# Building the gate table of a 128 x 128 expert grid: one-hot rows by Relu on ACT in place of compares on DVE

## The chip, the core and the metric

The kernel runs on one core of one Trainium2 chip. The metric is the device time in microseconds of one execution. TensorE appears in the profile as PE (matmuls) and PEld (weight loads), VectorE as DVE, ScalarE as ACT, GpSimd as POOL and SyncE, which only issues transfers, as SP.

## The reference, cut to what matters

One decoder layer is computed for 1024 prompt rows and 64 sample rows: norm, input projection, a recurrent branch and a windowed attention branch, a merge, an output projection, and then an expert layer with 8 heads that pick 16 experts each out of 128 x 128:

```python
s_top, i_top = lax.top_k(s, PEER_TOPK)                    # 16 of 128 keys on each of two axes
cand = s_top[:, :, 0, :, None] + s_top[:, :, 1, None, :]  # 16 x 16 sums
cand_idx = i_top[:, :, 0, :, None] * N_KEYS + i_top[:, :, 1, None, :]
best, pos = lax.top_k(cand, PEER_TOPK)
idx = jnp.take_along_axis(cand_idx, pos, axis=-1)         # expert numbers, 128 per token
g = jax.nn.softmax(best, axis=-1)                         # gates
act = jax.nn.gelu(jnp.einsum('cd,ced->ce', xc, expert_u[ic])) * gc
return jnp.einsum('ce,ced->cd', act, expert_v[ic])
```

For 704 of the 1088 tokens the kernel computes this layer densely, over all 16384 experts. For this it needs a gate table per token: a 128 x 128 array that holds the gate at row i, column j where expert 128 i + j was picked, and zero elsewhere.

## The kernel before

The rows are worked in three blocks: 320 rows (256 prompt and 64 sample rows), 384 and 384. A block goes through `trunk`: attention, gate and attention-branch projections (with `mg`), the recurrent part `lru`, its branch projection, the output projection `w_out`, the second norm (whose transposes on PE write the PSUM tile `tr`), and `retrieve`, which computes the key scores and the two top-16 lists. What a block's lists need after that is background work, done while the next block is in `trunk`: `choose` (top 16 of the candidate sums, expert numbers, softmax) and, for the first two blocks alone, `build_g`, which makes the gate tables. The 384 rows of the third block are gathered expert by expert during `dense`, the last and longest part (from 1912 us on), which reads the tables of the other 704 tokens.

The background work is a Python generator. `bg(k)` takes k steps of it at set places of `trunk` (`PG1` and `PG2` list how many), and so sets its place in the order of the program; a scheduler then orders each engine's queue. All tiles of one name share a ring of buffers that is given out in the order of the program. The PSUM tile `tr` has three buffers, used by the table products, by the key scores and by every transpose, those of the second norm too. A step of `build_g` makes the tables of four tokens, called a group here; 80 groups are built during the second block and 96 during the third.

A group before: DVE compares a row of the numbers 0 to 127 with the tokens' column numbers (line 889) and row numbers (line 890), giving one-hot rows for 4 tokens x 128 slots. The gate is held as a sum of three bf16 parts, so the row one-hots are multiplied by each part (line 891 on POOL, 892 and 893 on DVE). PE multiplies the one-hots, three 128 x 128 bf16 matmuls per token that add up in `tr` (lines 896 to 898), and ACT copies the result into `sg` (line 899). After eight groups (32 tokens) `sg` is stored to `g_d` with 2 MB (line 901). `sg` has one buffer.

In `choose`, line 786 compares 50 candidate places with the 16 picked places, POOL multiplies by the expert numbers (line 788), DVE adds up (line 789). In attention, line 443 scales the softmax on POOL. Weights come by SP (`wraw`), are split into a high part by ACT (`whi`, line 148) and a low part by POOL (`wlo`, line 149), and go to PE.

## Time and profile before

| what | value |
|---|---|
| median of 3 runs | 4001.42 us (3998.14 to 4010.92) |
| the profiled execution's own time | 3999.96 us |
| its span, from the first to the last instruction | 3998.0 us |
| PE busy | 3641.4 us, 91% of the span |
| DVE busy | 3151.0 us, 79% |
| POOL busy | 2407.2 us, 60% |
| ACT busy | 1290.8 us, 32% |

Busy time is summed over the whole span and so is a mean of stages with different limits. The first block lasts from 0 to 520 us, the second to 1232, the third to 1912, and `dense` to the end. The two middle stretches are 1392 us long, and the background work lies in them. A matmul's recorded duration includes the filling of the array, so several overlap; what one costs is read from one start to the next.

### The profile page before, as it was taken

Reading aid. Unit: us, or ns where it says so; the run is one execution under the profiler, and the core shown is the slowest. Engines: PE = TensorE matmul, PEld = TensorE weight load, DVE = VectorE, ACT = ScalarE, POOL = GpSimd, SP = SyncE. Lnnn points to the kernel's source line nnn. Section 1 sums busy time; section 2 is a strip of 40 time slices with the busy share of each in tenths; the row PEclk is TensorE's granted clock in tenths of the full one; section 3 lists DMA queues with packets and bytes.
Section 4 is the critical chain, followed back from the end, with each engine's and each line's share of the span. In section 5 each row is a group of like instructions: output and inputs, shape, how many; then the busy total and the mean of one; then the engine's idle time right before and its main releaser. Section 6 shows DMA issues by size and latency. Waiting matters only on the chain. (4 is left out here: it accounts for less than half of the span.)

```text
span 3998.0 us, 60600 instructions
## 1 busy us (share of the span) xinstructions
PE 3641.4 (91%) x22734; PEld 3477.6 (87%) x22734; DVE 3151.0 (79%) x6798; ACT 1290.8 (32%) x2346; POOL 2407.2 (60%) x1560
## 2 busy tenths in 40 slices
PE   7988998778897878998899999999999999999998
PEld 6778978668895777888799999999999999999998
DVE  6365787999899988998987777777777777777773
ACT  4454353443333435333222222222222222222221
POOL 3444546565554664764576677767766767676651
PEclk8989999889997988999899999999999999999999
DMA  5334523234441133444359898999989899899972
GB/s 148 100 111 149 154 72 90 79 101 145 171 139 56 58 94 108 138 173 162 125 204 308 292 318 303 321 323 316 322 295 311 306 319 316 309 317 310 319 259 80
DMA packets 505654, 821.75 MB, mean 206 GB/s; under 512 B 34220, under 2 KB 360812, under 8 KB 502000
## 3 DMA queue, kind: packets, MB, share of 16 engines
q1 hardware_dynamic: 394768, 415.18, 32.5%
q0 software_dynamic: 110592, 402.70, 28.2%
q8 instruction: 178, 2.92, 0.3%
q14 instruction: 116, 0.95, 0.1%
HBM read 753.25 MB, written 66.50 MB: 205 GB/s over the span
## 5 line engine op out<-in xcount | busy, mean ns | idle before, releaser
L149 POOL TENSOR_TENSOR wlo<-wraw,whi 128x1024 fp32r<-128x1024 f32 x252 | 639.3, 2544 | 513.7 <-ACT whi L148 476.0
L168 PE MATMUL ou<-ah,vh 128*128 128x352 f32 x2048 | 663.4, 327 | 40.6 <-ACT ah L148 23.3
L168 PE MATMUL sc<-dx,uh 128*128 128x352 f32 x2048 | 664.6, 325 | 16.2 <-ACT uh L148 9.0
L169 PE MATMUL ou<-al,vh 128*128 128x352 f32 x2048 | 660.1, 325 | 5.3 <-DVE al L149 5.0
L170 PE MATMUL sc<-dx,ul 128*128 128x352 f32 x2048 | 662.0, 323 | 1.0 <-POOL ul L149 1.0
L169 PE MATMUL sc<-dx,uh 128*128 128x352 f32 x2048 | 662.5, 324 | 0.0
L170 PE MATMUL ou<-ah,vl 128*128 128x352 f32 x2048 | 659.0, 324 | 0.0
L859 DVE SCALAR_TENSOR_TENSOR acc<-row,hv,acc 128x1024 f32<-128x1024 f32 x384 | 493.1, 1284 | 157.3 <-DMA row<-in_expert_v,iA 151.6
L847 DVE SCALAR_TENSOR_TENSOR row<-row,xt 128x1024 f32<-128x1024 f32 x384 | 465.5, 1217 | 174.3 <-DMA row<-in_expert_u,iA 165.0
L857 POOL DMA_INDIRECT row<-in_expert_v,iA x384 | 362.2, 943 | 267.8 <-DVE acc L859 192.6
L845 POOL DMA_INDIRECT row<-in_expert_u,iA x384 | 362.4, 944 | 264.4 <-DVE row L847 187.4
L168 PEld LDWEIGHTS ou<-ah,vh 128*128 128x128 f32 x2048 | 385.0, 189 | 55.7 <-ACT ah L148 29.7
L168 PEld LDWEIGHTS sc<-dx,uh 128*128 128x128 f32 x2048 | 386.9, 189 | 20.0 <-DVE al L149 9.8
L148 ACT CAST whi<-wraw 128x1024 fp32r<-128x1024 f32 x252 | 263.9, 1049 | 429.6 <-PE mm L169 167.6
L169 PEld LDWEIGHTS ou<-al,vh 128*128 128x128 f32 x2048 | 387.0, 189 | 7.8 <-DVE al L149 7.8
L170 PEld LDWEIGHTS sc<-dx,ul 128*128 128x128 f32 x2048 | 386.5, 189 | 1.4 <-POOL ul L149 1.4
L169 PEld LDWEIGHTS sc<-dx,uh 128*128 128x128 f32 x2048 | 387.2, 189 | 0.0
L170 PEld LDWEIGHTS ou<-ah,vl 128*128 128x128 f32 x2048 | 386.8, 189 | 0.0
L970 DVE TENSOR_TENSOR dac<-dac,ou 128x352 f32<-128x352 f32 x672 | 339.3, 514 | 59.9 <-PE ou L170 58.0
L149 POOL TENSOR_TENSOR vl<-vn,vh 128x1024 fp32r<-128x1024 f32 x128 | 309.0, 2422 | 65.6 <-ACT vh L148 38.5
L149 POOL TENSOR_TENSOR ul<-un,uh 128x1024 fp32r<-128x1024 f32 x128 | 310.7, 2427 | 45.7 <-ACT uh L148 43.6
L891 POOL TENSOR_TENSOR oij<-oij,s 128x512 bf16<-128x512 bf16 x176 | 225.1, 1290 | 176.9 <-DVE oij L890 132.7
(287 smaller groups left out, 8484.5 us busy)
## 6 DMA issues: line engine op xcount, KB each, us to landing
wraw<-in_w_in SPq DMA_DIRECT2D x132, 512.0 KB
un<-in_expert_uT SPq DMA_DIRECT2D x128, 512.0 KB
vn<-in_expert_v SPq DMA_DIRECT2D x128, 512.0 KB
g_d<-sg SPq DMA_DIRECT2D x22, 2048.0 KB
gt<-g_d SPq DMA_DIRECT2D x64, 704.0 KB
wraw<-in_peer_w_query SPq DMA_DIRECT2D x48, 512.0 KB
wraw<-in_w_branch_attn SPq DMA_DIRECT2D x24, 512.0 KB
wraw<-in_w_branch_lru SPq DMA_DIRECT2D x24, 512.0 KB
```

The lines of the kernel that those rows point to most:

```text
L148: nc.scalar.copy(hi, src)
L149: return (lo_eng or nc.vector).tensor_tensor(lo, src, f32(hi), op=ALU.subtract)
L168: nc.tensor.matmul(ps, lh, rh, start=first and j == 0, stop=False)
L169: nc.tensor.matmul(ps, lh, rl, start=False, stop=False)
L170: nc.tensor.matmul(ps, ll, rh, start=False, stop=last and j == n - 1)
L845: nc.gpsimd.indirect_dma_start(out=row, out_offset=None, in_=i["expert_u"], in_offset=bass.IndirectOffsetOnAxis(ap=ia[:, s:s + 1], axis=0))
L847: nc.vector.scalar_tensor_tensor(row, row, 1.0, xt, op0=ALU.mult, op1=ALU.mult, accum_out=hv[:, s:s + 1])
L857: nc.gpsimd.indirect_dma_start(out=row, out_offset=None, in_=i["expert_v"], in_offset=bass.IndirectOffsetOnAxis(ap=ia[:, s:s + 1], axis=0))
L859: nc.vector.scalar_tensor_tensor(acc, row, hv[:, s:s + 1], acc, op0=ALU.mult, op1=ALU.add)
L891: nc.gpsimd.tensor_tensor(wl, wh, col(4), op=ALU.mult)
L970: nc.vector.tensor_tensor(ac[k // 4][:, k % 4, a:b], ac[k // 4][:, k % 4, a:b], ps[:, 0:b - a], op=ALU.add)
```

## The change

The one-hot rows are no longer compared on DVE. For a slot with number s and a column c, the squared distance (s - c)^2 is written as a product of eight factors of s by eight factors of c, split so that each factor is exact in bf16. The slots' factors go to DRAM (`ft_d`), are read back eight tokens at a time with the eight factors on partitions (`fq`), and PE multiplies them by a constant 8 x 256 table (`fcmp`): 256 columns of distances per token, for the column and the row number. ACT then computes Relu(1 - d) for the column one-hots, and Relu(w - w d) for the row one-hots, with the gate w as a pointer operand for scale and for bias. One fp32 matmul per token multiplies both. The product of a group is issued after the distances of the next one. `choose` finds the expert number as the least of |32768 place + number - 32768 wanted|, with a subtract and a reduce on DVE and nothing on POOL. The softmax scaling in attention is four ACT instructions in place of one on POOL. Setup builds the constant table and takes it through DRAM.

```diff
+        row = self.sp.tile([1, NF, 2, P], BF16, tag="s4", name="row", bufs=N4)
...
+        nc.sync.dma_start(self.fc_d.rearrange("(o f) x c -> o f x c", o=1), row)
+        self.fcmp = c.tile([NF, 2 * P], BF16, name="fcmp")
+        nc.sync.dma_start(self.fcmp, self.fc_d.rearrange("f x c -> f (x c)"))
...
-            nc.gpsimd.tensor_tensor(sb[:, :, 0:S], sb[:, :, 0:S], z4.unsqueeze(2).to_broadcast([P, 4, S]), op=ALU.mult)
+            for g in range(4):
+                nc.scalar.activation(sb[:, g, 0:S], sb[:, g, 0:S], AF.Copy, scale=z4[:, g:g + 1])
...
+            nc.vector.tensor_tensor(ce[0:r], ce[0:r], self.iota[0:r].unsqueeze(1).to_broadcast([r, PH, NCAND]), op=ALU.add)
...
-                nc.vector.tensor_tensor(eq[0:r], self.iota[0:r].unsqueeze(1).to_broadcast([r, TOPK, NCAND]),
-                                        bf[0:r, h].unsqueeze(2).to_broadcast([r, TOPK, NCAND]), op=ALU.is_equal)
-                nc.gpsimd.tensor_tensor(eq[0:r], eq[0:r], ce[0:r, h].unsqueeze(1).to_broadcast([r, TOPK, NCAND]), op=ALU.mult)
-                nc.vector.tensor_reduce(ev[0:r, h], eq[0:r], axis=AX.X, op=ALU.add)
+                nc.vector.tensor_tensor(eq[0:r], ce[0:r, h].unsqueeze(1).to_broadcast([r, TOPK, NCAND]),
+                                        bf[0:r, h].unsqueeze(2).to_broadcast([r, TOPK, NCAND]), op=ALU.subtract)
+                nc.vector.tensor_reduce(ev[0:r, h], eq[0:r], axis=AX.X, op=ALU.min, apply_absolute_value=True)
...
+                nc.vector.tensor_scalar(x12[0:r, 0, 2], e32[0:r], 7, None, op0=ALU.arith_shift_right)
+                nc.vector.tensor_scalar(x12[0:r, 1, 2], e32[0:r], 127, None, op0=ALU.bitwise_and)
+                nc.vector.tensor_tensor(x12[0:r, :, 0], x12[0:r, :, 2], x12[0:r, :, 2], op=ALU.mult)
+                nc.vector.tensor_scalar(x12[0:r, :, 1], x12[0:r, :, 0], 127, None, op0=ALU.bitwise_and)
+                nc.vector.tensor_scalar(x12[0:r, :, 0], x12[0:r, :, 0], 7, None, op0=ALU.arith_shift_right)
+                nc.scalar.copy(fb[0:r, 0:6], x12[0:r].rearrange("p x f s -> p (x f) s"))
...
+                nc.sync.dma_start(self.ft_d[:, n0:n0 + r, :].rearrange("f n s -> n f s"), fb[0:r])
...
+        def product(ch, t4, sg, oij):
+            pt = self.tr()
+            for x in range(4):
+                nc.tensor.matmul(pt[:, x, :], oij[:, x, 1], oij[:, x, 0], start=True, stop=True)
+            nc.scalar.copy(sg[:, :, t4 * 4:t4 * 4 + 4], pt.rearrange("p x i -> p i x"))
+            if t4 == CH // 4 - 1:
+                nc.sync.dma_start(self.g_d[ch], sg)
...
-                nc.vector.tensor_tensor(oj, self.iota4, col(1), op=ALU.is_equal)
-                nc.vector.tensor_tensor(wh, self.iota4, col(0), op=ALU.is_equal)
-                nc.gpsimd.tensor_tensor(wl, wh, col(4), op=ALU.mult)
-                nc.vector.tensor_tensor(wm, wh, col(3), op=ALU.mult)
-                nc.vector.tensor_tensor(wh, wh, col(2), op=ALU.mult)
...
-                    nc.tensor.matmul(pt[:, x, :], oj[:, :, x], wh[:, :, x], start=True, stop=False)
-                    nc.tensor.matmul(pt[:, x, :], oj[:, :, x], wm[:, :, x], start=False, stop=False)
-                    nc.tensor.matmul(pt[:, x, :], oj[:, :, x], wl[:, :, x], start=False, stop=True)
...
+                    fq = sp.tile([NF, CF, NSLOT], BF16, tag="fq", name="fq", bufs=2)
+                    nc.sync.dma_start(fq, self.ft_d[:, n0:n0 + CF, :])
...
+                for x2 in range(2):
+                    ps = self.tr((P, 2, 2, P))
+                    for x in range(2):
+                        m = (t4 * 4) % CF + 2 * x2 + x
+                        nc.tensor.matmul(ps[:, x].rearrange("p a c -> p (a c)"), fq[:, m, :], self.fcmp, start=True, stop=True)
+                    nc.scalar.activation(oij[:, 2 * x2:2 * x2 + 2, 1, :], ps[:, :, 1, :], AF.Relu, scale=-1.0, bias=1.0)
+                    for x in range(2):
+                        m = t4 * 4 + 2 * x2 + x
+                        nc.scalar.activation(oij[:, 2 * x2 + x, 0, :], ps[:, x, 0, :], AF.Relu, scale=sw[:, 1, m:m + 1], bias=sw[:, 0, m:m + 1])
+                if late:
+                    product(*late.pop(0))
+                late.append((ch, t4, sg, oij))
                 yield
```

The order of the queues. First PE in the third block, where the last background groups meet the first transpose of the second norm (`xn`); `oij` are the one-hots, `tr` the shared PSUM tile. Before:

```order
L896 LDWEIGHTS oij_17693
L896 MATMUL tr_17699<-oij_17693 128x128
L897 LDWEIGHTS oij_17693
L897 MATMUL tr_17699<-oij_17693 128x128
L898 LDWEIGHTS oij_17693
L898 MATMUL tr_17699<-oij_17693 128x128
L239 MATMUL tr_17741<-ident_60,xn_17722 128x128 [waits DVE_49,Activation_49]
L239 MATMUL tr_17741<-ident_60,xn_17722 128x128 x3
```

Now, at the same place:

```order
L936 LDWEIGHTS fq_17566 [waits PE_49]
L936 MATMUL tr_17684<-fcmp_226,fq_17566 128x256 [waits Activation_49]
L936 LDWEIGHTS fq_17566
L936 MATMUL tr_17684<-fcmp_226,fq_17566 128x256
L912 MATMUL tr_17690<-oij_17568 128x128 [waits Activation_49]
L912 MATMUL tr_17690<-oij_17568 128x128 x3
L263 MATMUL tr_17724<-ident_60,xn_17705 128x128 [waits DVE_49,PE_49,Activation_49]
L263 MATMUL tr_17724<-ident_60,xn_17705 128x128 x3
```

Each pair of distance matmuls and each product now takes a buffer of `tr` and waits for ACT. Of the third block's 96 groups, 66 stood ahead of the first `w_out` matmul before and 30 between it and the retrieval; now 41 and 55, of which 43 stand back to back with no projection between. Of the second block's 80 groups, 30, 28 and 22 stood in the recurrent branch's projection, in `w_out` up to the retrieval, and in the retrieval; now 2 come earlier, and 16, 39 and 23 there.

Then ACT in the same part of the third block; `sg` is the table tile that is stored after eight groups, `whi` a weight's high part. Before:

```order
L899 COPY sg_16664<-tr_16679 128x128x4 [waits DMAHW3_49,Activation_49]
L899 COPY sg_16664<-tr_16699 128x128x4
L899 COPY sg_16664<-tr_16719 128x128x4
L148 CAST whi_17603<-wraw_17605 128x1024 [waits DMAHW1_49,PE_49]
L899 COPY sg_16664<-tr_16805 128x128x4 [waits PE_49]
L899 COPY sg_16664<-tr_16825 128x128x4 [waits PE_49]
```

Now:

```order
L940 ACTIVATE oij_17202<-tr_17203,sw_17189 128x128 x2
L937 ACTIVATE oij_17202<-tr_17209 128x2x128 [waits PE_49]
L940 ACTIVATE oij_17202<-tr_17209,sw_17189 128x128 x2
L937 ACTIVATE oij_17215<-tr_17216 128x2x128 [waits PE_49,Activation_49]
L940 ACTIVATE oij_17215<-tr_17216,sw_17189 128x128 x2
L937 ACTIVATE oij_17215<-tr_17222 128x2x128 [waits PE_49]
L940 ACTIVATE oij_17215<-tr_17222,sw_17189 128x128 x2
L937 ACTIVATE oij_17348<-tr_17349 128x2x128 [waits PE_49,Activation_49]
L940 ACTIVATE oij_17348<-tr_17349,sw_17189 128x128 x2
L937 ACTIVATE oij_17348<-tr_17355 128x2x128 [waits PE_49]
L940 ACTIVATE oij_17348<-tr_17355,sw_17189 128x128 x2
L913 COPY sg_17201<-tr_17228 128x128x4 [waits DMAHW2_49,Activation_49]
```

ACT has six Relu instructions per group beside the copy, and the first copy of a new `sg` waits for the store of the one before; three groups' Relu instructions stand ahead of that copy.

Last SP at the start, where the constant table is taken through DRAM (`fc_d`, `fcmp`) between the weight loads. Before:

```order
L204 DMA wraw_540<-in_w_in 128x4x256 [waits DMAHW6_49,Pool_49]
L204 DMA wraw_654<-in_w_in 128x4x256 [waits DMAHW7_49,DMAHW4_49,Pool_49]
L204 DMA wraw_660<-in_w_in 128x4x256 [waits DMAHW5_49,DMAHW0_49,Pool_49]
L204 DMA wraw_774<-in_w_in 128x4x256 [waits DMAHW6_49,DMAHW1_49,Pool_49]
L204 DMA wraw_780<-in_w_in 128x4x256 [waits DMAHW7_49,DMAHW2_49,Pool_49]
```

Now:

```order
L228 DMA wraw_561<-in_w_in 128x4x256 [waits DMAHW6_49,Pool_49]
L117 DMA fc_d_68<-row_207 1x2048 [waits DMAHW7_49,DVE_49]
L119 DMA fcmp_226<-fc_d_68 8x256 [waits DMAHW7_49,DMAHW0_49]
L228 DMA wraw_675<-in_w_in 128x4x256 [waits DMAHW4_49,DMAHW1_49,Pool_49]
L228 DMA wraw_681<-in_w_in 128x4x256 [waits DMAHW5_49,DMAHW2_49,Pool_49]
```

The read of `fcmp` waits for the landing of its write, and the weight loads behind it wait with it. Later the 88 loads of `fq` and the 22 of `sw` stand between weight loads in the same queue.

## Rows read from the trace of the kernel before

**Rows 1.** Busy time per stretch: start:end, length, engines, granted PE clock, DMA share, GB/s.

```profile
core 0: us, PE busy (x) PEld busy (x) DVE busy (x) ACT busy (x) POOL busy (x), PEclk, DMA share, GB/s
221.00:334.00 113.00, 90.03 (x487) 79.23 (x486) 85.26 (x189) 71.18 (x125) 42.83 (x17) 0.85 0.36 108
334.00:384.00 50.00, 45.98 (x302) 45.50 (x301) 23.46 (x45) 19.06 (x28) 32.72 (x14) 0.93 0.50 151
640.00:854.00 214.00, 164.13 (x808) 150.88 (x808) 201.57 (x428) 91.95 (x136) 131.51 (x57) 0.88 0.28 82
854.00:966.00 112.00, 97.74 (x659) 93.22 (x660) 105.36 (x182) 36.22 (x62) 77.42 (x43) 0.89 0.42 134
966.00:1083.00 117.00, 96.20 (x790) 92.85 (x789) 112.37 (x236) 40.82 (x71) 69.92 (x42) 0.94 0.48 169
1083.00:1232.00 149.00, 138.82 (x955) 134.06 (x954) 131.62 (x494) 51.15 (x88) 69.21 (x39) 0.97 0.43 138
1232.00:1443.00 211.00, 164.07 (x764) 130.39 (x765) 200.92 (x551) 78.56 (x203) 128.47 (x62) 0.84 0.18 53
1443.00:1747.00 304.00, 259.90 (x1685) 242.21 (x1683) 272.41 (x431) 135.15 (x218) 179.38 (x100) 0.91 0.40 134
1747.00:1830.00 83.00, 69.02 (x570) 67.20 (x568) 77.09 (x159) 27.96 (x47) 42.94 (x31) 0.88 0.51 177
1912.00:2045.00 133.00, 113.26 (x644) 108.75 (x645) 130.23 (x380) 38.20 (x55) 87.73 (x41) 0.92 0.32 104
```

**Rows 2.** Groups by line, DVE: shapes and count, busy us, mean ns, idle before.

```profile
L893 DVE TENSOR_TENSOR oij<-oij,s 128x512 bf16<-128x512 bf16 x176 | 156.0, 902 | 7.2 <-POOL oij L891 7.1
L892 DVE TENSOR_TENSOR oij<-oij,s 128x512 bf16<-128x512 bf16 x176 | 127.7, 743 | 0.2
L889 DVE TENSOR_TENSOR oij<-iota,s 128x512 bf16<-128x512 bf16 x176 | 114.6, 651 | 27.1 <-PE tr L898 27.0
L786 DVE TENSOR_TENSOR eq<-iota,bf 128x800 f32<-128x800 f32 (+1 forms) x72 | 100.9, 1411 | 0.4
L890 DVE TENSOR_TENSOR oij<-iota,s 128x512 bf16<-128x512 bf16 x176 | 100.2, 569 | 0.0
```

**Rows 3.** Line 786 alone: duration min/median/max in ns, first and last start.

```profile
L786 DVE TENSOR_TENSOR eq<-iota,bf x72: 964/990/3216, 650.9 to 2038.3; 128x800 f32<-128x800 f32 x64, 64x800 f32<-64x800 f32 x8
```

**Rows 4.** Groups by line, POOL: the multiply of a group.

```profile
L891 POOL TENSOR_TENSOR oij<-oij,s 128x512 bf16<-128x512 bf16 x176 | 225.1, 1290 | 176.9 <-DVE oij L890 132.7 <-DVE s L883 26.2 <-DVE rs_tk L183 6.0
```

**Rows 5.** Groups by line, PEld: one weight load of a table product.

```profile
L897 PEld LDWEIGHTS <-oij 128*128 128x128 bf16 x704 | 84.5, 120 | 22.7 <-issue 21.7
```

**Rows 6.** Timeline of PE from 722.5 us: start, length of the row, count.

```profile
722.64 0.34 PE L170 MATMUL mm<-xh,wlo 128*128 128x384 f32 x1
722.82 0.81 PE L643 MATMUL mm<-xc,wa 128*128 128x384 f32 x2
```

**Rows 7.** Groups by line and shape, ACT: copies from PSUM, without and with pointer operands.

```profile
L899 ACT COPY sg<-tr 128x512 f32<-128x512 f32 x176 | 100.0, 586 | 186.4 <-PE tr L898 163.7 <-DMA g_d<-sg 18.3 <-issue 4.0
L649 ACT ACTIVATE q<-T,sm 128x384 f32<-128x384 f32 x16 | 11.3, 708 | 2.1 <-DVE xc L630 1.9
L362 ACT COPY qn<-mm 128x256 f32<-128x256 f32 x26 | 9.7, 372 | 22.4 <-PE mm L170 22.2
L315 ACT ACTIVATE gh<-mg 128x384 fp32r<-128x384 f32 x16 | 7.0, 512 | 1.2 <-DVE mg L308 1.2
L569 ACT COPY pT<-tr 128x128 f32<-128x128 f32 x8 | 2.0, 265 | 3.5 <-PE tr L568 3.4
```

**Rows 8.** Timeline of ACT at 908 us, two copies back to back.

```profile
908.89 1.07 ACT L899 COPY sg<-tr 128x512 f32<-128x512 f32 x2
```

**Rows 9.** Timelines of SP and ACT: a store of `sg`, and the next copy into it.

```profile
886.77 0.34 SPq L901 DMA_DIRECT2D g_d<-sg  x1
...
894.34 1.19 ACT L899 COPY sg<-tr 128x512 f32<-128x512 f32 x2 [6.07 <-DMA g_d<-sg]
```

**Rows 10.** Waits of ACT: total us, times, longest.

```profile
ACT whi L148 <- DMA wraw<-in_w_in: 20.1, 5, 11.9
```

More of the change, by code (lines that the diff above doesn't have):

```diff
@@ L38 @@
 NCAND = len(PAIRS)
+STEP = 32768
 SLOPES = [float(np.float32(2.0) ** np.float32(-8.0 * (h + 1) / NH)) for h in range(NH)]
@@ L63 @@
 CH = 32
+NF = 8
+CF = 8
 def f32(ap):
@@ L824, in slots_T @@
         nc = self.nc
-        pt = self.tr((P, 3, P))
-        for x in range(3):
-            nc.tensor.transpose(pt[:, x, 0:r], ft[0:r, x], self.ident[0:r, 0:r])
-        sl = self.xp.tile([P, 3, P], F32, tag="sl", name="sl", bufs=1)
-        nc.scalar.copy(sl[:, :, 0:r], pt[:, :, 0:r])
-        nc.sync.dma_start(self.sT_d[:, :, n0:n0 + r], sl[:, :, 0:r])
+        pt = self.tr((P, P))
+        nc.tensor.transpose(pt[:, 0:r], ft[0:r], self.ident[0:r, 0:r])
+        sl = self.xp.tile([P, P], F32, tag="sl", name="sl", bufs=1)
+        nc.scalar.copy(sl[:, 0:r], pt[:, 0:r])
+        nc.sync.dma_start(self.sT_d[:, n0:n0 + r], sl[:, 0:r])
     def gather_steps(self, gp, gps):
@@ new lines, in build_g @@
+        late = []
+        def product(ch, t4, sg, oij):
[5 more added lines that the diff above has]
+                nc.sync.dma_start(self.g_d[ch], sg)
+        for ch in range(ROW0[bi] // CH, (ROW0[bi] + n) // CH):
+            sw = sp.tile([P, 2, CH], F32, tag="sw", name="sw", bufs=2)
+            nc.sync.dma_start(sw[:, 0], self.sT_d[:, ch * CH:(ch + 1) * CH])
+            nc.scalar.activation(sw[:, 1], sw[:, 0], AF.Copy, scale=-1.0)
+            for t4 in range(CH // 4):
+                if t4 % (CF // 4) == 0:
+                    n0 = ch * CH + t4 * 4
+                    fq = sp.tile([NF, CF, NSLOT], BF16, tag="fq", name="fq", bufs=2)
+                    nc.sync.dma_start(fq, self.ft_d[:, n0:n0 + CF, :])
+                if t4 == 0 and late:
+                    product(*late.pop(0))
+                if t4 == 0:
+                    sg = sp.tile([P, AT], F32, tag="at", name="sg", bufs=1)[:, 0:P * CH].rearrange("p (i n) -> p i n", i=P)
+                oij = self.sp.tile([P, 4, 2, P], F32, tag=self.otag, name="oij", bufs=N4 if self.otag == "s4" else 6)
+                for x2 in range(2):
[4 more added lines that the diff above has]
+                    nc.scalar.activation(oij[:, 2 * x2:2 * x2 + 2, 1, :], ps[:, :, 1, :], AF.Relu, scale=-1.0, bias=1.0)
+                    for x in range(2):
+                        m = t4 * 4 + 2 * x2 + x
+                        nc.scalar.activation(oij[:, 2 * x2 + x, 0, :], ps[:, x, 0, :], AF.Relu, scale=sw[:, 1, m:m + 1], bias=sw[:, 0, m:m + 1])
+                if late:
+                    product(*late.pop(0))
+                late.append((ch, t4, sg, oij))
@@ L902, in build_g @@
                 yield
+        for u in late:
+            product(*u)
     def dense_x(self):
```

54 lines of the change are left out of this document (25 added, 29 removed).

## The prediction

> **What bounds the kernel now.** I read the 40 slices of the page first: from 2000 us on PE is at nine tenths or more, before that PE, DVE and the granted clock all sag, so the change can move the time only in the two middle blocks and in the start of `dense`. Then I cut these blocks into stretches by the lines that stand in them. The reader is to see in [rows 1] that from 640 to 1443 and from 1443 to 1830 DVE is the fullest engine almost throughout: 201.6 of 214 us, 105.4 of 112, 112.4 of 117, 200.9 of 211, 272.4 of 304, 77.1 of 83. PE has 69 to 98 us in the same short stretches and is granted 0.84 to 0.94 of its clock, ACT has a third or less. In the first block, which has no background work, the same part of the program (the projections at 334 to 384) keeps PE at 46 of 50 us with DVE at 23. So the middle blocks are limited by DVE, and what fills it there is the gate table. The second view, the groups by line, gives its price: four passes of 651, 569, 743 and 902 ns, 2.87 us of DVE per group of four tokens [rows 2], and 1.29 us of POOL [rows 4].
>
> **What the group costs after the change.** On DVE nothing, on POOL nothing. On PE it had twelve matmuls whose weight loads follow each other every 0.12 us [rows 5], 1.44 us. Now there are four with 128 bf16 weight columns and 256 moving ones, and four fp32 ones. For the first I keep 0.12. For the second: the trace has two fp32 matmuls of 384 columns in 0.81 us, so at most 0.41 each and 0.14 for 128 columns, while the row above them starts 0.18 before [rows 6]; I take 0.12 again. A group is then 8 x 0.12 = 0.96 us of PE, 0.5 less than now.
>
> The rule in the Trainium skill (FP8 and Floating Point Precision, TensorE Precision Notes) that true FP32 takes four passes through the array speaks against this product. The trace disagrees: by that rule two matmuls of 384 columns need an estimated 1.28 us at 2.4 GHz for their columns alone, and they took 0.81 [rows 6]. By the Trainium skill an fp32 product would cost an estimated 0.2 us, a group 0.35 us more, which counts only in the stretches that PE limits, some 20 us in all; I leave it out.
>
> On ACT the group had one copy. Now it has that copy, two Relus of 256 elements with constants, and four Relus of 128 elements with two pointer operands. The trace has no Relu. A copy of 256 elements from PSUM takes 372 ns and one of 128 takes 265 [rows 7]; the exponential with pointers for scale and bias takes 708 where a copy of the same 384 elements with a constant takes 512, so two pointers cost 0.2 us [rows 7], and I price the small Relu at 0.465. Two copies of 586 ns end after 1.07 us [rows 7, 8], so 0.10 us of each overlaps with the next. A full ACT queue then passes a group in 4 x 0.365 + 2 x 0.27 + 0.485 = 2.48 us. The bounds: 1.68 if pointers cost nothing here, 3.19 if nothing overlaps. I take the middle value, which is nearest to how such rows stand in this trace.
>
> The Trainium skill speaks against the move (ScalarE: Activation LUTs, Rules for kernel authors): Relu is to go to VectorE, which is faster per element. Its figures for ACT (same page, What ACT_TABLE_LOAD costs) are 186 ns and 0.833 ns per element with constants, 93 ns more per pointer, 93 ns of overlap, an estimate of 2.7 us a group. The copy of 256 in [rows 7] is 27 ns under that, so I keep the rows; by the Trainium skill the sum below would end some 20 us later.
>
> So ACT takes over where DVE stood, with 2.48 us for 2.87, and it has far less other work. What decides is where the groups now stand. The order puts fewer groups beside the projections and more of them, 43 in a row in the third block, between `w_out` and the second norm, and the norm's transposes must wait for them, since all use the ring `tr`. There PE and ACT have nothing else, and the pace is ACT's. The store of `sg` adds to it: from issue to the next copy are 7.57 us, of which ACT idles 6.07 [rows 9]; three groups' Relus stand ahead of that copy now, 3 x 2.0 = 6.0 us, which leaves 1.6 us per eight groups.
>
> **The sum,** by stretches of [rows 1], against the profiled execution's 3999.96 us:
>
> - 640 to 854 (`choose`, recurrent part): DVE-bound. 24 compares at a mean of 1.41 us beside POOL's multiply [rows 2] fall to the median 0.99 [rows 3], 10 us; the added passes of three tiles (800 elements take 0.99, so 400 take half, and some six short ones, each under the 0.57 of line 890 [rows 2], so 4 to 12 us for three tiles) cost 7; two groups' passes that were run ahead go, 6. **-9.**
> - 854 to 966: the first block's stretch took 50 us at 320 rows, so 60 at 384; 16 groups on PE add 15. 75 for 112, **-37.** ACT has 19 + 40 us there, and stays under.
> - 966 to 1083, 39 groups: ACT has 40.8 - 28 x 0.59 = 24 us of its own, 39 x 2.48 = 97, stores 5 x 1.6 = 8. 129 for 117, **+12.**
> - 1083 to 1232 (retrieval, 23 groups): PE has 138.8; 32 of matmuls leave, 22 come, and about half of its 10 idle us, which DVE caused, go. **-15.**
> - 1232 to 1443: DVE at 200.9. As in the first line -3 for `choose`, and six groups' passes run ahead, 6 x 2.87 = 17. **-20.** Nine groups now come here, 22 us of ACT on 79; the softmax scaling adds 48 instructions of about 0.4, 19 us. There is room.
> - 1443 to 1747, 32 groups: the first block took 113 + 50 = 163 us, 196 at 384 rows; 32 x 0.96 = 31 on PE. 227 for 304, **-77.** ACT: 95 of its own and 79, 174 of 227.
> - 1747 to 1830, 55 groups: ACT 28 - 30 x 0.59 = 10 of its own, 136, stores 7 x 1.6 = 11. 157 for 83, **+74.**
> - 1912 to 2045 (`choose` of the third block beside `dense`, DVE at 130 of 133): 24 compares lose 0.42 each, 10, two for the added pass. **-8.** The rest of `dense` is PE's and stays.
> - Start: two more transfers in SP's queue, each waiting for a landing, with three loads of weights ahead of them. Between 0 and 15 us, since a 2 MB store lands in 7.57 [rows 9]; two such small ones behind prefetched weights, **+2.**
>
> Together -9 - 37 + 12 - 15 - 20 - 77 + 74 - 8 + 2 = -78, so 3922 us. The profiled execution lies 1.5 under the median of the runs shown, which I don't correct for.
>
> **The rivals.** *ACT is cheaper.* If pointers cost nothing on a PSUM source, a group passes in 1.68. The third stretch then falls from 129 to 24 + 66 + 5 x 4 = 110 (less Relu work covers the store), the one before the end of the third block from 157 to 10 + 92 + 7 x 4 = 130. That is 46 less, 3876. For it: a copy of 128 takes only 265 [rows 7]. Against it: the 708 against 512. Lower still it could go if the recurrent parts, at 0.88 to 0.91 of the clock, gain clock as PE fills.
>
> *No change.* The two ACT-paced stretches hold 94 groups. At 78 / 94 = 0.83 us more per group, 3.3 in place of 2.48, they give back all that the others win, 4000. For it: full durations make 3.19. Against it: [rows 8] shows the overlap.
>
> *Slower: the ACT queue stalls.* ACT works in order, so a Relu that waits for PE holds the weights' `whi` casts and PE waits for these. If nothing overlaps (3.19) and the store is not covered (7.57 / 8 = 0.95), a group costs 4.14 against the 2.69 that I used (2.48 and 0.21 of store), 1.45 x 94 = 136 more, 4058. It decides from 3.5 us a group on. For it: ACT did idle 6.07 of the 7.57 us. Against it: the order has three groups' work ahead of each such copy.
>
> *Slower: SP's queue.* The loads of `fq` wait for PE to release their buffer, with weight loads behind them. ACT waited five times for a weight so far, 4 us each [rows 10]. If each of the 22 chunks caused one such wait, 88 us, the time would be 4010. Against it: weights are loaded three tiles ahead.
>
> **Chances.** Forecast 0.56, cheaper ACT 0.22, no change 0.08, stalled ACT 0.08, SP's queue 0.06. About 0.3%, 12 us, is what a measurement of this kernel tells from no change. So faster 0.78, same 0.08, slower 0.14. The forecast's own range, with a group between 2.2 and 3.0 us, is 3895 to 3975; with the rivals that hold 8 in 10 it is 3840 to 4005, below the cheap case because the recurrent parts may gain more, above up to where ACT or SP just loses.
>
> **What would show it.** In the profile after: DVE at two thirds or less in the stretches of both blocks' projections; the stretch between `w_out` and the second norm's transposes of the third block twice as long as now, with ACT nearly full and one group every 2.5 to 2.7 us; the recurrent part and its projection of the third block some 75 us shorter; the product's fp32 matmuls 0.11 to 0.14 us apart; idle time of `sg`'s first copies under 2 us. The forecast is wrong if the small Relus take over 0.55 us each or stand apart, if ACT waits for weights more than now, or if the stretches that I took from the first block stay as long as they are because something else than DVE held them.

## The result and the profile after

The changed kernel takes 4058.45 us (median of 4 runs, 4047.84 to 4062.89) where the kernel before, run beside it, takes 3999.78 (4 runs, 3997.92 to 4010.92). The ratio is 1.014, interval 1.0119 to 1.0161: slower by 59 us, where 78 faster were forecast. The profiled execution has a span of 4059.2 us against 3998.0.

The first view after is that of [rows 1], with its columns, cut at the marks of the new trace (the first sum of the attention branch, of `w_lru`, of `w_out`, the last sum of `w_out`, the last transposes of the second norm, the last key scores).

```profile
core 0: us, PE busy (x) PEld busy (x) DVE busy (x) ACT busy (x) POOL busy (x), PEclk, DMA share, GB/s
658.00:859.00 201.00, 170.08 (x893) 154.36 (x892) 178.86 (x469) 109.73 (x187) 86.13 (x34) 0.93 0.34 100
859.00:943.00 84.00, 82.45 (x509) 70.95 (x508) 15.83 (x24) 57.05 (x131) 36.48 (x15) 1.00 0.48 156
943.00:1094.00 151.00, 136.36 (x878) 111.19 (x876) 27.56 (x94) 119.45 (x306) 26.31 (x12) 0.85 0.37 130
1094.00:1259.00 165.00, 150.91 (x969) 131.06 (x968) 71.01 (x398) 95.57 (x217) 52.25 (x22) 0.97 0.44 140
1259.00:1458.00 199.00, 164.82 (x781) 127.56 (x782) 150.72 (x552) 108.82 (x288) 43.14 (x17) 0.85 0.19 56
1458.00:1697.00 239.00, 227.27 (x1327) 191.57 (x1326) 94.97 (x126) 188.07 (x412) 82.19 (x34) 0.99 0.41 137
1697.00:1741.00 44.00, 43.76 (x341) 37.72 (x341) 8.19 (x29) 31.99 (x76) 13.15 (x6) 1.00 0.49 169
1741.00:1875.00 134.00, 119.56 (x508) 89.44 (x507) 8.86 (x26) 110.97 (x302) 3.45 (x2) 0.56 0.33 122
```

DVE is no longer the fullest engine anywhere but in the first row: 15.8 of 84 us where it had 105.4 of 112, 95.0 of 239 where it had 272.4 of 304. PE is full beside the projections, at a granted clock of 0.99 to 1.00. But the last row is new. It is the 134 us between `w_out` and the second norm of the third block, in which almost nothing but groups of the gate table runs: PE is busy for 119.6, ACT for 111.0, and PE is granted 0.56. In the row above it, up to 1741 us, PE had 1.00.

The same marks in both traces give this ledger, in us (the two last columns are the difference and what the prediction had):

| stretch, to the mark | before | after | diff. | forecast |
|---|---|---|---|---|
| first sum of the second block's attention branch | 631.5 | 658.4 | +27 | +2 |
| first sum of `w_lru` | 222.7 | 200.5 | -22 | -9 |
| first sum of `w_out` | 121.0 | 83.9 | -37 | -37 |
| last transposes of the second norm | 107.2 | 151.1 | +44 | +12 |
| last key scores | 149.1 | 165.2 | +16 | -15 |
| last sum of the third block's attention branch | 210.0 | 199.0 | -11 | -20 |
| first sum of `w_out` | 314.6 | 238.9 | -76 | -77 |
| last transposes of the second norm | 73.7 | 190.5 | +117 | +74 |
| last key scores | 80.6 | 81.0 | 0 | 0 |
| end | 2087.6 | 2090.7 | +3 | -8 |

The gains came nearly to the microsecond. The losses were forecast too small, and in four places. The groups by line say what a group costs now; the columns are those of [rows 2].

```profile
L912 PE MATMUL tr<-oij 128*128 128x128 f32 x1408 | 244.9, 330 | 15.7 <-ACT oij L940 11.4 <-ACT sg L913 3.3 <-DVE yl L173 0.5
L936 PE MATMUL tr<-fcmp,fq 8*128 8x256 bf16 x704 | 145.2, 309 | 15.0 <-ACT oij L940 6.4 <-ACT sg L913 5.0 <-DVE yl L173 1.7
L940 ACT ACTIVATE oij<-tr,sw 128x128 f32<-128x128 f32 x704 | 289.8, 477 | 0.0
L937 ACT ACTIVATE oij<-tr 128x256 f32<-128x256 f32 x352 | 139.7, 397 | 52.9 <-PE tr L936 52.2
L913 ACT COPY sg<-tr 128x512 f32<-128x512 f32 x176 | 104.5, 594 | 57.8 <-PE tr L912 54.6 <-DMA g_d<-sg 2.4
L815 DVE TENSOR_REDUCE ev<-eq 128x16 f32<-128x800 f32 (+1 forms) x72 | 68.7, 969 | 0.0
```

176 groups have 704 products, but the first row counts 1408 instructions: one fp32 matmul is two on PE, each with its own weight load. The copy into `sg` waited for its store for 2.4 us in all, for the product 54.6. One group of the new row, on the timeline (start, length, count, in brackets the idle time before):

```profile
1798.85 1.03 PE L936 MATMUL tr<-fcmp,fq 8*128 8x256 bf16 x4
1798.95 0.59 ACT L913 COPY sg<-tr 128x512 f32<-128x512 f32 x1 [0.38 <-PE tr L912]
1799.49 0.38 ACT L937 ACTIVATE oij<-tr 128x256 f32<-128x256 f32 x1
1799.77 0.80 ACT L940 ACTIVATE oij<-tr,sw 128x128 f32<-128x128 f32 x2
1799.81 2.08 PE L912 MATMUL tr<-oij 128*128 128x128 f32 x8
1800.45 0.39 ACT L937 ACTIVATE oij<-tr 128x256 f32<-128x256 f32 x1
1800.72 0.83 ACT L940 ACTIVATE oij<-tr,sw 128x128 f32<-128x128 f32 x2
1801.92 0.59 ACT L913 COPY sg<-tr 128x512 f32<-128x512 f32 x1 [0.38 <-PE tr L912]
```

From one copy to the next are 2.97 us, and that is the median of the whole stretch; with the change to a new `sg`, eight groups take 25.1 us, 3.14 each. ACT's part is near what was forecast: 1798.95 to 1801.55 is 2.6 us with the tail of the last Relu. Where its queue is full, the median distance to the next start is 0.48 us after a copy, 0.28 after a large Relu and 0.34 after a small one, which makes 2.4 for a group. Here it waits 0.38 more for the product. PE has no such gap: four distance matmuls and eight product instructions follow each other, nine of the twelve about 0.21 us after the one before and three, around the changes from one kind to the other, 0.35 to 0.37, together 2.97. In the retrieval, where PE has its full clock, the same eight take half:

```profile
1156.66 1.05 PE L912 MATMUL tr<-oij 128*128 128x128 f32 x8
```

The waits (engine, line, what it waited for: us, times, longest; the first line is the kernel before) show who stands behind the row. The second norm's `yl` does, which had waited 3.1 us in all before, and POOL's cast of the weights behind ACT's. They are idle time and no price by themselves.

```profile
POOL wlo L149 <- ACT whi L148: 476.0, 136, 21.9
POOL wlo L173 <- ACT whi L172: 1225.9, 207, 150.6
DVE yl L173 <- ACT yh L172: 192.3, 8, 126.9
```

### The profile page after: what moved, and what is told of

Read it like the earlier page. It is cut to its first block, busy times and chain, and to the rows that moved or that the text cites. A ratio compares the mean times of both kernels' runs of the same rounds, so it can differ in the third digit from the quotient of the medians.

```text
span 4059.2 us, 60731 instructions
## 1 busy us (share of the span) xinstructions
PE 3767.1 (93%) x22722; PEld 3488.0 (86%) x22722; DVE 2591.3 (64%) x6047; ACT 1685.6 (42%) x3535; POOL 1962.8 (48%) x1280
## 5 line engine op out<-in xcount | busy, mean ns | idle before, releaser
L173 POOL TENSOR_TENSOR wlo<-wraw,whi 128x1024 fp32r<-128x1024 f32 x252 | 621.0, 2469 | 1331.8 <-ACT whi L172 1225.9
L172 ACT CAST ah<-sc 128x352 fp32r<-128x352 f32 x256 | 115.8, 453 | 553.8 <-DVE sc L994 553.8
```

Of the source, the lines that this page charges most:

```text
L172: nc.scalar.copy(hi, src)
L173: return (lo_eng or nc.vector).tensor_tensor(lo, src, f32(hi), op=ALU.subtract)
```

## The experiments

"Period" below is the median distance of two copies into `sg` between the last sum of `w_out` and the second norm in the third block, the row of 40 groups or so; the change to a new `sg`, once in eight groups, is not in it. Ratios are to the kernel before, run on the same chip.

**The product in bf16, and in F32R,** a 4-byte format to which the gate is then rounded.

```diff
-oij = self.sp.tile([P, 4, 2, P], F32, ...)
+oij = self.sp.tile([P, 4, 2, P], BF16, ...)    # second kernel: F32R
```

> The changed kernel with both factors of the product written as bf16, so that a product is one PE instruction in place of two; the gate is rounded to bf16 (that part of the computation is changed). Theory A (the fp32 product was mis-priced: eight instructions per group, 2.0 us at the lower clock, set the pace of the backlog with ACT behind it): the group's period between w_out and the second norm falls from 2.97 to 2.5-2.6 us, 52 groups by 0.4 = 20 us there, and the stretches that PE limits lose 0.45 us per group, some 20-40 us more; total 4000-4020. Rival B (ACT alone sets the pace): the period stays at 2.9-3.0 and the total over 4045.

> The changed kernel with the product's factors written as F32R (the gate is rounded to that format, which changes this part of the computation a little). Theory A (what made the product dear is that an fp32 matmul is two PE instructions of two passes each; an F32R one is a single instruction like the bf16 one): a product takes 0.1-0.15 us at full clock, total 4000-4020, as with bf16. Rival B (128 moving columns of F32R are no cheaper than fp32): total 4045-4060.

bf16: 4008.58 us, ratio 1.001 (0.9995 to 1.0025); F32R: 4031.45, ratio 1.0072 (1.0044 to 1.0100). The periods are 2.38 and 2.37. Each product is one instruction again, x704 in both. The windows of the row, bf16 and then F32R:

```profile
1726.00:1836.00 110.00, 68.51 (x326) 32.60 (x325) 8.33 (x24) 102.63 (x294) 2.88 (x2) 0.52 0.39 144
```

```profile
1728.00:1844.00 116.00, 89.08 (x335) 55.63 (x333) 11.15 (x26) 105.35 (x300) 5.38 (x2) 0.51 0.38 140
```

Here ACT is full, 102.6 of 110 us, and the period is its own. F32R, which takes away the second PE instruction of each product, was worth 27 us by the medians, between the totals of both theories. bf16 was worth 50: with it the instruction is shorter too. At the full clock the product's instructions start 0.06 us apart with bf16, 0.11 with F32R, and 0.11 with fp32, where there are two. The clock stayed low.

**Half of the Relus, then all of them, on VectorE,** with the fp32 product.

```diff
-nc.scalar.activation(oij[..., 1, :], ps[:, :, 1, :], AF.Relu, scale=-1.0, bias=1.0)
+nc.vector.tensor_scalar(oij[..., 1, :], ps[:, :, 1, :], 0.0, None, op0=ALU.is_equal)
 # second kernel also, with the softmax scaling on GpSimd:
-nc.scalar.activation(oij[..., 0, :], ps[:, x, 0, :], AF.Relu, scale=sw[:, 1, m:m + 1], bias=sw[:, 0, m:m + 1])
+nc.vector.tensor_scalar(oij[..., 0, :], ps[:, x, 0, :], 0.0, sw[:, 0, m:m + 1], op0=ALU.is_equal, op1=ALU.mult)
```

> The changed kernel with one of the two kinds of Relu, the 256-element one with constants, on VectorE instead of ACT (a comparison with 0 gives the same ones), the product in fp32 as it was. ACT's part of a group falls from 2.48 to about 1.9 us, PE's stays. Theory A (between w_out and the second norm PE at half of its clock sets the period, eight product instructions of 0.25 and four distance matmuls of 0.24 make 2.96): the period stays at 2.8-3.0 us, total 4045-4060. Rival B (ACT sets it): the period falls to about 2.4, 52 groups by 0.55 = 29 us, total 4020-4035.

> As the kernel with all Relus on VectorE and the scaling on GpSimd, but with the product in fp32 as in the changed kernel (nothing is rounded). Theory A (what PE is granted in a row of groups follows from how much it has to do between VectorE's or ACT's passes: with 1.5 us of VectorE per group and 1.34 of PE its clock stays up): clock over 0.85 between w_out and the second norm, period 1.6-1.9 in place of 2.01, total 3970-3995. Rival B (the clock is low in every row of groups that has no projections): clock about 0.5, period 2.9-3.0 as in the changed kernel, total 4040-4075.

4069.28 us (1.0171, 1.0146 to 1.0195) and 4036.12 (1.0079, 1.0055 to 1.0103). The period is 2.97 in both. The row's windows, the first kernel's and then the second's:

```profile
1763.00:1897.00 134.00, 119.85 (x504) 89.50 (x503) 40.74 (x109) 89.52 (x219) 2.74 (x2) 0.55 0.32 122
```

```profile
1754.00:1866.00 112.00, 104.14 (x431) 77.62 (x431) 67.98 (x241) 22.49 (x42) 0.81 (x1) 0.52 0.34 127
```

ACT fell from 111 of 134 us to 22 of 112 and not a hundredth of the period went. It is PE's, at half of its clock. Theory A of the second kernel, that a fuller PE would get its clock back, fell: PE is 93% busy there at 0.52. (The first kernel's 11 us over the changed one lie within the two intervals; in its profile the first copy into `sg` comes at 816 us in place of 791, and 32 groups in place of 27 stand behind `w_out` in the second block.) VectorE's Relus of one group, from the second kernel's timeline:

```profile
1799.94 0.41 DVE L936 TENSOR_SCALAR oij<-tr 128x256 f32<-128x256 f32 x1
1800.28 0.60 DVE L939 TENSOR_SCALAR oij<-tr,sw 128x128 f32<-128x128 f32 x2
1800.79 0.41 DVE L936 TENSOR_SCALAR oij<-tr 128x256 f32<-128x256 f32 x1
1801.12 0.60 DVE L939 TENSOR_SCALAR oij<-tr,sw 128x128 f32<-128x128 f32 x2
1801.64 0.41 DVE L936 TENSOR_SCALAR oij<-tr 128x256 f32<-128x256 f32 x1
```

From 1799.94 to 1801.64 are 1.7 us, and the next group's begin.

**All Relus on VectorE with the F32R product** (the two edits above, the F32R tile, and the scaling on GpSimd).

> The changed kernel with all Relus of the gate table on VectorE (comparison with 0, times the weight, from PSUM), the product in F32R (gate rounded to it) and the softmax scaling on GpSimd. ACT has only the copy of 0.59 us per group, VectorE about 1.5. Theory A (where groups stand in a row, PE at half of its clock sets the pace: four distance matmuls of 0.24 and four products of 0.25-0.3): the period falls from 2.38 of the F32R kernel to about 2.0-2.1, 45 + 30 groups by 0.3, and ACT's queue is free: total 3995-4015. Rival B (ACT set the 2.38 and VectorE takes its place with 1.5 us): period 1.5-1.7, total 3960-3985. Rival C (the Relus on VectorE collide with the scans and the score tables): period as in A, but the recurrent part longer by 20 us or more, total over 4030.

3983.44 us, ratio 0.9957 (0.9940 to 0.9973), period 2.01. Theory A, a little better in total. PE's eight instructions fill the period, the products 0.21 us apart, the distance matmuls 0.19, and more around the changes of kind.

**More work on PE.** The changed kernel with each product matmul issued twice; and the F32R kernel with VectorE's Relus (and the scores' ring of below) with each distance matmul issued twice.

```diff
+for _ in range(2):
     nc.tensor.matmul(pt[:, x, :], oij[:, x, 1], oij[:, x, 0], start=True, stop=True)
```

> The changed kernel with each product matmul issued twice into the same place (same result). Theory A (PE at half clock sets the period of a row of groups, and its clock stays low): the period between w_out and the second norm rises from 2.97 by eight instructions of 0.25 to about 5 us, total 4170-4200. Rival B (PE at the full clock is far from the limit, and more work on it brings the clock up): the granted clock of that stretch rises from 0.56 to over 0.9, the period falls to ACT's 2.5, total 4030-4060. Rival C (ACT sets the period, PE has room even at half clock): period about 3.0, total 4060-4080.

> The same with each distance matmul issued twice into the same place (same result). Theory A (more work on PE between VectorE's passes brings its clock up, as the doubled product did): clock between w_out and the second norm over 0.85 in place of 0.50, period 1.5-1.7 in place of 2.01; the stretches that PE fills pay 0.44 us per group, about 30; total 3950-3970. Rival B (the clock stays low): period 2.9-3.0, total over 4030.

4132.14 us (1.0310, 1.0279 to 1.0342) and 4022.14 (1.0043, 1.0028 to 1.0058). The rows' windows:

```profile
1833.00:1951.00 118.00, 101.43 (x718) 85.00 (x717) 10.93 (x29) 93.39 (x254) 4.67 (x2) 0.91 0.31 117
```

```profile
1731.00:1838.00 107.00, 100.05 (x422) 67.86 (x422) 71.20 (x239) 22.50 (x41) 2.50 (x2) 0.50 0.37 132
```

With eight more instructions per group the first kernel's row got faster: the clock rose to 0.91 and the period fell from 2.97 to 2.73. On the timeline of that row sixteen product instructions now take what eight took:

```profile
1891.98 2.05 PE L913 MATMUL tr<-oij 128*128 128x128 f32 x16
```

So the low clock is the cause of the 2.97 and no companion of it. At 0.91 PE no longer sets the pace, and ACT, at 93 of 118 us, doesn't either: the copy waits for its product, and the next product for that copy, whose buffer of `tr` it takes.

```profile
1891.34 0.59 ACT L914 COPY sg<-tr 128x512 f32<-128x512 f32 x1 [0.18 <-PE tr L913]
1891.97 1.86 PEld L913 LDWEIGHTS tr<-oij 128*128 128x128 f32 x16 [0.42 <-ACT sg L914]
```

2.05 and 0.59 us in turn, with 0.09 between them, are the 2.73. So theory B had the clock, but not the period nor the total, which rose as PE had eight instructions more in each group of the other stretches too. The doubled distance matmul raised nothing: clock 0.50, period 2.86, which is 2.01 and four instructions of 0.21, near rival B. Which matmuls bring the clock up, and which don't, stays open; I tried no more of them.

Eight of the kernels together, PE instructions being those of a group; the last column is the median distance in us from one instruction of the product to the next, in the row:

| kernel | Relus, us per group | PE instr. | clock | period | set by | product instr. |
|---|---|---|---|---|---|---|
| changed kernel | ACT 2.4 with the copy | 12 | 0.56 | 2.97 | PE | 0.21 |
| half of the Relus on VectorE | ACT 1.9 with the copy | 12 | 0.55 | 2.97 | PE | 0.21 |
| all on VectorE, fp32 | VectorE 1.7 | 12 | 0.52 | 2.97 | PE | 0.21 |
| bf16 product | ACT 2.4 with the copy | 8 | 0.52 | 2.38 | ACT | 0.11 |
| F32R product | ACT 2.4 with the copy | 8 | 0.51 | 2.37 | ACT | 0.21 |
| all on VectorE, F32R | VectorE 1.7 | 8 | 0.50 | 2.01 | PE | 0.21 |
| the same, distance twice | VectorE 1.7 | 12 | 0.50 | 2.86 | PE | 0.21 |
| product twice | ACT 2.4 with the copy | 20 | 0.91 | 2.73 | product and copy in turn | 0.11 |

**Groups elsewhere.** If a group is dear in a row of its own, it may be cheap beside the retrieval's projections: by another pace, or by another PSUM ring, so that the norm need not wait.

```diff
-PG2 = (6, 6, 5, 1, 2, 4, 2, 2)
+PG2 = (6, 6, 2, 0, 0, 4, 2, 2)
 # the other kernel, for both tiles of build_g:
-ps = self.tr((P, 2, 2, P))
+ps = self.pp.tile([P, 2, 2, P], F32, tag="po", name="ps", bufs=2)
```

> The changed kernel with another pace of the background steps in the third block: (6,6,2,0,0,4,2,2) in place of (6,6,5,1,2,4,2,2), so that 24 groups stand between w_out and the second norm in place of 55, and 31 in the retrieval; the ring is shared as before. Theory A: 31 x 2.97 = 92 us leave the stretch before the norm, 31 x 1.4 = 43 come back in the retrieval, total about 4010. Rival B (a group costs the same wherever it stands, since ACT and the ring pace it): the retrieval grows by what the other stretch loses, total 4050-4060.

> The changed kernel with the PSUM tiles of the gate table (distances and product) in the two buffers of the attention's output ring, not in the ring that the norm's transposes use. In the program 19 + 3 groups then stand between w_out and the second norm of the third block in place of 52 + 3, and 43 in its retrieval; in the second block 59 stand in the retrieval in place of 23. Theory A (groups cost 2.97 us each where nothing else runs, and 1.3-1.6 us where PE is full): 33 x 2.97 = 98 us leave the one stretch, 43 x 1.4 = 60 come back in the retrieval, and the second block gains about 20: total about 4000. Rival B (a group costs ACT's 2.5-3.0 us wherever it stands, or two buffers are too few): total 4045 or more.

4078.71 us (1.0205, 1.0168 to 1.0243) and 4155.98 (1.0384, 1.0351 to 1.0418). Both theories A fell. With the other pace the stretch before the norm lost 88 us, but the retrieval went from 69 to 178 us, 109 for 31 groups, 3.5 each. It has two halves:

```profile
1811.00:1900.00 89.00, 87.13 (x527) 75.46 (x526) 17.62 (x96) 54.19 (x128) 27.00 (x12) 1.00 0.34 104
1900.00:1988.00 88.00, 68.18 (x257) 49.56 (x256) 44.76 (x267) 41.30 (x111) 0.00 (x0) 0.55 0.17 70
```

The projections ran first, at the full clock, and what remained were groups and scores in a row of their own again, at 0.55. In the kernel with its own ring 58 groups stood between `w_out` and the first key score, and with two buffers the period was 3.8 (the clock from 1900 to 1950 was 0.50).

**The scores in another ring than the groups.**

```diff
-s = self.tr((P, P))
+s = self.pp.tile([P, P], F32, tag="po", name="s", bufs=2)
```

> The changed kernel with the retrieval's key scores in the two buffers of the attention's output ring, not in the ring of the gate table. Theory A (in the retrieval a group costs 3.5 us since scores, which VectorE holds for five passes, and the group's three tiles wait for each other in one ring): the second block's retrieval, 148 us with 21 groups, falls to 115-125, total 4030. Rival B (order and clock set it, the groups come behind the projections in a row): 143-150, total within 8 us of 4058.

4088.12 us, ratio 1.0212 (1.0184 to 1.0241). Where groups and scores stand together it did what A says: the second block's retrieval fell from 148 to 114 us. It lost more in the two retrievals without groups, 73 to 104 and 69 to 87 us, where the scores now had two buffers in place of three. So the ring is taken for the second block alone below (`if bi == 1`).

> The kernel with all Relus on VectorE, an fp32 product and the scaling on GpSimd, and with the second block's key scores in the ring of the attention's output. Theory A: its retrieval is 25-35 us shorter than without, as it was with ACT's Relus (148 to 114), total that much under the kernel without it. Rival B (with the Relus on VectorE it is VectorE's 64 + 21 x 1.5 = 96 us that bound the stretch, together with PE's): 10 us or less.

> The kernel before with the new choice of the expert number (3974.6), and with the second block's key scores in the ring of the attention's output, where that block alone has groups of the gate table in its retrieval. Theory A (the shared ring makes a group dear there): the second block's retrieval falls from 138 us with 20 groups by 15-30, total 3945-3960. Rival B (there VectorE's four passes per group, 57 us, and the scores' five, 64, are the limit): within 5 us of 3974.

With the fp32 product and VectorE's Relus: 4015.09 us (1.0029, 1.0013 to 1.0044), 21 under the same without it, and the retrieval 119 us for 143, a little less than A. With the old gate table: 3975.90 (0.9925, 0.9900 to 0.9951) for 3974.55, so nothing; its retrieval fell from 138 to 130 only.

**The single parts.** The choice of the expert number by least distance alone, put into the kernel before; the same with the softmax scaling on ACT; and the changed kernel with that scaling back on GpSimd.

> The kernel before with one part of the change alone: the expert number by the least distance (one subtraction and one reduction on VectorE, no multiply on GpSimd); gate table and softmax as before. Theory A (the prediction's term: 24 passes per block of the middle that fall from 1.41 to about 1.0 us while VectorE bounds the stretch, and as much in the third block beside the dense part): 10 us each in three blocks, less 1 us each for the added pass, total 3970-3980. Rival B (VectorE's idle time elsewhere swallows it, the compare was slow only because GpSimd ran beside it): within 8 us of 4000.

> The kernel before with the new choice of the expert number and with the softmax scaling on ACT, the gate table as before. Against the kernel with the new choice alone (3974.6) it shows the scaling by itself, where no row of groups takes up what is gained or lost ahead of it. Theory A (the scaling on ACT costs the first block 8 us and the two others as much, since ACT's queue feeds the transposes of the scores): 3985-3998. Rival B (it is hidden): 3970-3980.

> The changed kernel with one part undone: the softmax scaling is one GpSimd multiply per score tile again, not four ACT passes. Theory A (the first block's 17 us come from this part: ACT got 11 us more of queue in the attention, and 6 come from the setup of the constant table): the end of the first block's key scores moves from 538 us back to about 527, the gap before the merge of the second block (9 us more than before) closes too, total about 4040. Rival B (the scaling was hidden, and the first block is longer by the clock that PE was granted): the block's end stays at 538 and the total within 5 us of 4058.

The choice alone: 3974.55 us, ratio 0.9943 (0.9925 to 0.9962), 24 us faster, as A has it. With the scaling on ACT 3978.38 (0.9941, 0.9918 to 0.9965), no difference that the runs can tell, though the two profiled executions are 10 us apart (3965.5 and 3975.5). The changed kernel without it: 4053.86 (1.0136, 1.0104 to 1.0167), 5 us less, within the intervals again. What is left for the gate table is 4058 - 3975 = 83 us, less the 0 to 10 of the scaling.

**The constant rows of the distance product built later,** with the scaling on GpSimd.

```diff
 def build_g(self, bi):
+    if bi == 0:
+        self.table_rows()       # the block of setup that made row and fcmp
```

> The changed kernel with the softmax scaling on GpSimd again and with the constant rows of the distance product built at the start of the first gate table, not in the setup ahead of the first block. Theory A (the setup's rows and their two transfers hold the first block up by 4 to 8 us): the last transposes of the first norm end at 27 us in place of 31, the first block's key scores end at 521-524 us in place of 530, total 4044-4048. Rival B (something else in the setup, or the order of the first loads): the end stays at 528-532, total 4050-4056.

4060.06 us, ratio 1.0159 (1.0135 to 1.0184). The first block gained more than A says, 12 us for 4 to 8. First and last start of its key scores (range behind the durations), before, after, after with GpSimd's scaling, and with that and the late rows:

```profile
L732 PE MATMUL tr<-skT,qr x96: 270/273/377, 448.6 to 521.4; 128*128 128x128 f32 x64, 128*64 128x128 f32 x32
```

```profile
L757 PE MATMUL tr<-skT,qr x96: 270/273/377, 465.3 to 538.1; 128*128 128x128 f32 x64, 128*64 128x128 f32 x32
```

```profile
L756 PE MATMUL tr<-skT,qr x96: 270/273/377, 457.0 to 530.0; 128*128 128x128 f32 x64, 128*64 128x128 f32 x32
```

```profile
L739 PE MATMUL tr<-skT,qr x96: 270/273/377, 445.1 to 517.7; 128*128 128x128 f32 x64, 128*64 128x128 f32 x32
```

8 us are the scaling's, 12 the rows' and their transfers', which this run doesn't tell apart. Yet the total did not move: the second norm's last transposes of the second block start at 1091.5 us, where they started at 1093.9 with both losses. The first copy into `sg` came at 842 us in place of 791, as the rows were now built ahead of it, and 32 groups in place of 27 stood behind `w_out`, where the stretch to those transposes took 126 us in place of 105. So here the row took what had been won ahead of it; what the start is worth with the first groups in their old place this run doesn't show.

**What it adds up to:** VectorE's Relus, the F32R product (the gate is rounded to it), GpSimd's scaling, the scores of the second block in the other ring.

> The kernel with all Relus on VectorE, the product in F32R (gate rounded to it) and the scaling on GpSimd (3983.4), with the second block's key scores in the ring of the attention's output. Theory A (the shared ring is worth 24 us there, as with the fp32 product): retrieval of the second block from 147 to about 122 us, total 3955-3965, under both kernels and under the one with the new choice alone (3974.6). Rival B (with the shorter product the ring was no longer the limit): 3975-3985.

3955.71 us, ratio 0.9881 (0.9861 to 0.9901), under the kernel before, under the changed one and, by the ratios, under the choice alone (0.9943). Its retrieval in the second block and its row of groups:

```profile
1090.00:1205.00 115.00, 115.00 (x757) 100.71 (x756) 102.57 (x493) 42.02 (x70) 42.97 (x18) 1.00 0.43 143
1684.00:1777.00 93.00, 78.55 (x304) 47.39 (x304) 74.77 (x261) 23.74 (x44) 0.00 (x0) 0.50 0.46 173
```

The retrieval has PE full at its full clock; the row is still at half of it.

## Why the prediction was wrong

*What bound the kernel before* was right. With DVE relieved, the stretches beside the projections fell as forecast, -37 for -37 and -76 for -77, and the recurrent part by 13 more. (ACT had 32 to 44% of the stretches of [rows 1] that the prediction calls DVE's, not "a third or less".)

*The price of a group on PE* failed. The prediction read two fp32 matmuls in the "x2" of [rows 6] and said of the product "I take 0.12 again". The row is one matmul. Line 643 of the kernel before stands 48 times in its trace, where the program has 24:

```profile
L643 PE MATMUL mm<-xc,wa x48: 430/486/1009, 234.8 to 1592.9; 128*128 128x384 f32 x32, 128*128 128x320 f32 x16
```

The weight loads' 0.12 of [rows 5] is the length of one, too, and not a distance, but came near: the old product's matmuls start 0.118 us apart. A product of the new kernel is two instructions of 0.11 us at full clock, and a group 4 x 0.12 + 8 x 0.11 = 1.4 us in place of 0.96. The Trainium skill's rule of four passes for true FP32 (FP8 and Floating Point Precision, TensorE Precision Notes), which I rejected on that row, agrees with this trace: by it 128 columns need an estimated 0.21 us at 2.4 GHz, and two instructions of 0.11 us are 0.22.

*"The pace is ACT's"* failed. ACT's price was right, 2.4 us measured for 2.48 forecast. The copies waited for the store for only 2.4 us in all, where 19 had been put in, though a new `sg` still adds 1.3 us to eight groups (25.1 for 8 x 2.97). But PE was priced at its full clock, which it had wherever projections ran beside the groups. In the row of groups it was granted 0.56, and twelve instructions there take 2.97. That this sets the pace is shown by the two kernels that took Relus off ACT without any effect on the period, and by the one with the doubled product.

*The place of the groups* was read from the order, 43 in a row, but the sum let `w_out` run beside all 55 of its stretch. In fact `w_out` took its 44 us with 9 of them, and 46 came behind it in 147 us, the last four between the norm's transposes: 190.5, forecast 157. At the forecast's 2.69 the 46 would have taken 124, so about 23 of the 33 us are the price; the other 10 are that `w_out` took 44 us with its 9 groups and not 10 + 9 x 2.69 = 34. The same holds in the second block: 46 us of `w_out` with 10 groups, then 27 groups, 151 in place of 129.

*The retrieval* failed, +16 for -15. It was summed by PE's busy time alone. Groups and scores use one ring of three tiles, three per group and one for each score, which VectorE holds for its passes; a group cost (148 - 69) / 21 = 3.7 us there, and with the scores elsewhere (114 - 69) / 21 = 2.1.

*The start* failed, +27 for +2 up to the second block's attention branch. The two transfers were weighed, not VectorE's work on one partition beside the first norm (12 us at the end of the first block for both together), nor ACT's queue in the attention (8). At this mark the two kernels above show 18 us for the scaling and 11 for the rows (658.4, 640.2, 629.1). In the runs, though, neither moved the end of the program by what it cost in its place; the late rows also put off the first groups.

*The end:* the 8 us came (the first sum of the dense part starts 100 us after the last scores, 108 before), and 12 us were lost again over the 1962 us that follow. In the profiles of the kernels with the same `dense` the stretch from the last scores to the end lasts 2077 to 2105 us, so these 12 are within its scatter.

Two rivals named the sign. The stalled ACT queue, at 4058 us, had the time right by accident: its 4.14 us per group, uncovered stores and Relus without overlap, are refuted by the 2.97 us per group, the 2.4 us of waiting in all and ACT's 2.4 us per group. SP's queue, at 4010, is not borne out either: ACT waited for weights of `w_in` for 7.8 us in 4 waits, where it had been 20.1 in 5. It did wait for the new loads of `sw`, the gates of 32 tokens, which no term of the sum had; what that cost the end stays open.

```profile
ACT whi L172 <- DMA wraw<-in_w_in: 7.8, 4, 4.7
ACT sw L920 <- DMA sw<-sT_d: 26.8, 15, 6.9
```

## What to carry to other kernels

Price a step at the clock that the engine will have where the scheduler puts it: here work that fitted beside a full PE cost PE twice as much in a row of its own. Before a rate is read off a row of the timeline, count its instructions against the program's; in this case that would have doubled the product's price. When a gain and a loss stand in one change, try the parts alone: the smaller edit of three was worth 24 us, and the largest cost about 80.

## What was not expected of the hardware

- PE 89 to 93% busy with small matmuls for over 100 us was granted 0.50 to 0.56 of its clock throughout, that is mostly the 1.2 GHz level. Eight more fp32 instructions per group brought 0.91 and a shorter row; four more distance matmuls, of 8 rows by 256 columns, brought nothing.
- An fp32 matmul appears as two PE instructions, each with a weight load: 0.11 us at the full clock and 0.21 at half for 128 columns, against one instruction with F32R (0.11 and 0.21) or bf16 (0.06 and 0.11).
- The table product of the kernel before, three bf16 matmuls per token, had its matmuls 0.118 us apart at either level, the medians of 1690 pairs at the full clock and of 332 at half. (Its operands' columns lay four elements apart; whether that is the reason no run shows.) The change thus also gave up a product that the lower clock did not touch.
- VectorE made the one-hot rows from PSUM in 1.7 us per group, where ACT's Relus need 1.9 (2.4 with the copy).
